# A two-layer mixer with 32 routed experts per layer: expert weights loaded by 512 rows instead of 256

## The chip, the core and the metric

The kernel runs on one core of one Trainium2 chip, in float32. Five engines work side by side: TensorE (PE, with its weight loads PEld), VectorE (DVE), ScalarE (ACT), GpSimd (POOL) and SyncE (SP), which here issues nearly all transfers from device memory into the on-chip buffers. Sixteen DMA engines carry the transfers out. The metric is device microseconds (us) of one execution. Before the change it is 1542.18 us, the median of three runs (1540.11 to 1542.83).

## What is computed

Two layers are run over 256 tokens `x` and 256 context tokens `ctx` of width 1024. Each layer has a mixer (layer 0 a gated recurrence beside a spatial gating unit, layer 1 an attention with compressed keys) and then a mixture of 32 experts with two experts per token. Layer 0's experts see all 512 tokens, layer 1's only the 256 of `x`. The change is in the experts:

```python
def expert_block(args):                       # of hier_moe
    xb, e = args
    g, u = jnp.split(xb @ w_gu[e], 2, axis=-1)
    return (jax.nn.silu(g) * u) @ w_dn[e]
# w_gu: (2, 32, 1024, 1024), w_dn: (2, 32, 512, 1024), both float32
```

One expert has 4 MB of gate and up weights and 2 MB of down weights, so a layer has 192 MB, and both layers 384 MB of the 495 MB that the kernel moves.

## The kernel before

`body` runs `even_layer`, `moe` for layer 0, `odd_layer`, and `moe` for layer 1. In `moe` each expert has room for 64 token rows (`CAP`); what does not fit is left to `overflow`, which runs only if a count read from the data is positive.

**Steps.** `step(p)` (L1118) handles experts 2p and 2p+1; there are 16 steps a layer. It does `gate_up` for the first expert (L908: eight slices of the 1024 inputs, the stationary operand a slice of the gathered tokens `xT`, the moving one a weight row for each partition, 512 columns into each half of a PSUM bank), then for the second, then either `gather` (L871, which collects the tokens of the next four experts by a matmul with one-hot rows) or `combine` (L1039, which adds the finished outputs of four experts to the tokens), then `turned` (transposes the hidden rows), and `down` (L1019). PE's order is the order of the code (`manual_schedule`); for the other engines a planner chooses the order from a simulated run, SP's transfers included.

**Loads.** A load (`load_to`, L833) is 1 MB: 256 rows of one expert, two neighbouring rows on each partition, so 8 KB in one piece on each of 128 partitions. Twelve loads make a step: four and four of gate and up, two and two of down. Load number i goes into a slot of the pool `turn[i % len(turn)]` (L825 to L830). The pools are `wpb` and `wpa` (two 1 MB slots each, which the mixers use too), `wxa` (five slots in layer 0, eight in layer 1, L710 and L1433), `wxb` (four), and in layer 1 one slot `xcp`, in which `ctx` lay: 13 slots in layer 0, 17 in layer 1. A slot can be loaded again when the last matmul that reads it has ended. In layer 0 the list is turned so that load 191 ends it, and load 0 lies in `wpa`.

**Channels.** Row f of the down weights belongs to hidden channel f. With two neighbouring rows on a partition, `gate_up` puts channels 0 to 255 into one half of its PSUM bank and 256 to 511 into the other (`"p (a c n) -> p c a n"`, L914), each as one run of columns, and `turned` takes every second column (`h[par][:, j:256:2]`, L935).

**The test in the middle.** After step 11 of layer 0 and step 5 of layer 1 (`MID`), the kernel tests whether `overflow` must run:

```python
i = len(loads)
while turn[i % len(turn)] is not wpa:
    i += 1
load_to(i)
n = nc.values_load(nx[0:1, 0:1], min_val=0, max_val=15)
with tc.If(n > 0):
    overflow(n)
```

So loads are taken up to, and without, the first one that would go into `wpa`, since `overflow` uses `wpa` for its own weights. Later loads stand behind the test in the program, and a `wpa` slot is free for them only when PE is past it.

Of the kernel before, what the change touches and what calls it, by code (L numbers as in the profile page):

```python
# [16 lines left out]
D = 1024  # L17
# [8 lines left out]
def body(ctx, tc, I, out, dbg=None, stop=None):  # L26
# [305 lines left out]
    def even_layer(HL, main):  # L332
# [6 lines left out]
        with ExitStack() as st:  # L339
# [370 lines left out]
            wst, wxa = open_wxa(0, 5)  # L710
# [26 lines left out]
            ahead.append(load(W_out[:, 512:1024], wxa[-1]))  # L737
# [72 lines left out]
    def moe(R, wxa, nwb, out=None):  # L810
# [5 lines left out]
        with ExitStack() as st:  # L816
# [8 lines left out]
            n_load = 6 * NE  # L825
            if l == 0:
                turn = [wpb] * 2 + [wpa] * 2 + wxa + [wxb] * nwb
                turn = [turn[(i - n_load) % len(turn)] for i in range(len(turn))]
            else:
                turn = [wpb] * 2 + [wpa] * 2 + wxa + [xcp] + [wxb] * nwb  # L830
            loads = []

            def load_to(n):  # L833

                for i in range(len(loads), min(n, n_load)):
                    p, j = divmod(i, 12)
                    e, j, src = (2 * p + j // 4, j % 4, I["moe_w_gu"]) if j < 8 else (2 * p + (j - 8) // 2, j % 2, I["moe_w_dn"])
                    w = turn[i % len(turn)].tile([128, 2, D], F32, name="w")
                    if i >= n_load - 4:

                        c = (i - n_load + 4) // 2
                        v = w.rearrange("p k (h n) -> p (k h) n", h=2)
                        for e in range(2):
                            nc.sync.dma_start(v[:, 2 * e:2 * e + 2],
                                              src[l, NE - 2 + e, j * 256:(j + 1) * 256, c * 512:(c + 1) * 512]
                                              .rearrange("(p k) n -> p k n", p=128))
                        loads.append(v)
                        continue
                    nc.sync.dma_start(w, src[l, e, j * 256:(j + 1) * 256, :].rearrange("(p k) n -> p k n", p=128))
                    loads.append(w)  # L850
# [20 lines left out]
            def gather(P, xT, q0=0, q1=4):  # L871
# [36 lines left out]
            def gate_up(xT, base, wg):  # L908
# [34 lines left out]
            def gate_up_both(xT, wg):  # L943

                gus = [Q("gu") for _ in range(2)]
                for j in range(4):
                    w_ = wg(j)
                    for par in range(2):
                        for k in (2 * j, 2 * j + 1):
                            w = w_[:, k % 2, :].rearrange("p (a c n) -> p c a n", a=2, c=2)  # L950
# [12 lines left out]
            def finish(hT, w, PT, ws, fg, z):  # L963
# [6 lines left out]
                for c in range(2):  # L970
                    cs_ = slice(c * 512, (c + 1) * 512)
                    for k in range(4):
                        for par in range(2):
                            mm(py[c][64 * par:64 * par + 64, :], hT[par][:, k // 2, k % 2, :],  # L974
                               w[2 * c + k // 2][:, 2 * par + k % 2, :], start=k == 0, stop=k == 3)
# [27 lines left out]
            def settle(hT, w, PT, ws):  # L1003
# [3 lines left out]
                for c in range(2):  # L1007
                    for k in range(4):
                        for par in range(2):
                            mm(py[c][64 * par:64 * par + 64, :], hT[par][:, k // 2, k % 2, :],  # L1010
                               w[2 * c + k // 2][:, 2 * par + k % 2, :], start=k == 0, stop=k == 3)
# [7 lines left out]
            def down(hT, wd, ws, gated=False):  # L1019

                py = [Q("dn") for _ in range(2)]
                for j in range(2):
                    w_ = wd(j)
                    for k in (2 * j, 2 * j + 1):
                        for c in range(2):
                            for par in range(2):
                                mm(py[c][64 * par:64 * par + 64, :], hT[par][:, k // 2, k % 2, :],  # L1027
# [450 lines left out]
```

## Time and profile before

| | |
|---|---|
| median of three runs | 1542.18 us |
| the profiled execution | 1538.64 us, of which 1536.9 us from first to last instruction |
| busy: PE, PEld, DVE, ACT, POOL | 93%, 54%, 43%, 28%, 15% of the span |
| moved | 495.22 MB, mean 322 GB/s |
| layer 0's experts | about 402 to 890 us |
| layer 1's experts | about 1074 to the end |

A busy PE counts matmuls whose ends are modelled, and neighbouring matmuls overlap in the trace. The 1.7 us between the profiled execution's time and its span lie around the instructions.

### The profile page before, as it was taken

How to read it: one execution, taken by the hardware profiler on the slowest of the kernel's cores; microseconds unless marked ns; L12 is line 12 of the kernel's file. 1: busy time of each engine (PE TensorE's matmuls, PEld its weight loads, DVE VectorE, ACT ScalarE, POOL GpSimd, SP SyncE). 2: the span in 40 equal slices, each digit the busy share in tenths (PEclk: the TensorE clock that was granted, in tenths of full speed). 3: DMA queues.
4: the chain of work that ended last, by engine and by line, in shares of the span. 5: the costliest groups of instructions: out<-in, count | busy, mean ns of one | idle time of the engine just before them, and what ended most of it. 6: DMA issues, size and time to landing. Idle time of an engine off the chain costs nothing. (4 is left out here: it accounts for less than half of the span.)

```text
span 1536.9 us, 21613 instructions
## 1 busy us (share of the span) xinstructions
PE 1435.8 (93%) x8526; PEld 836.2 (54%) x8526; DVE 662.7 (43%) x1494; ACT 432.5 (28%) x984; POOL 224.9 (15%) x250
## 2 busy tenths in 40 slices
PE   6989999999799999999999988997999989999987
PEld 5767777868444554554535356886344434334443
DVE  4455546767424334244423455666232323222222
ACT  4433334543111111211112144453122212212212
POOL 2222222123002012022203221101010100010010
PEclk9999999999899999999999999998999999999999
DMA  9775344785899999999899853135999999999995
GB/s 354 230 248 162 114 144 159 289 298 202 352 406 420 419 421 419 419 420 420 362 417 381 334 226 104 53 99 204 404 420 420 420 419 421 420 421 420 420 420 207
DMA packets 126051, 495.22 MB, mean 322 GB/s; under 512 B 17739, under 2 KB 38636, under 8 KB 77816
## 3 DMA queue, kind: packets, MB, share of 16 engines
q1 hardware_dynamic: 119704, 487.33, 80.3%
q10 hardware_dynamic: 2192, 3.72, 0.7%
q0 software_dynamic: 4048, 2.73, 0.6%
q8 instruction: 70, 1.15, 0.3%
q14 instruction: 37, 0.30, 0.1%
HBM read 492.59 MB, written 1.13 MB: 321 GB/s over the span
## 5 line engine op out<-in xcount | busy, mean ns | idle before, releaser
L916 PE MATMUL gu<-w,xT 128*64 128x512 f32 x2048 | 456.6, 597 | 19.1 <-DMA w<-in_moe_w_gu_dram 13.2
L916 PEld LDWEIGHTS gu<-w,xT 128*64 128x64 f32 x2048 | 151.6, 138 | 313.5 <-issue 273.6
L1027 PE MATMUL dn<-w,hh 128*64 128x512 f32 x960 | 220.2, 606 | 0.0
L924 DVE COPY hh<-gu 128x256 f32<-128x256 f32 x64 | 27.2, 425 | 363.2 <-ACT junk L923 363.2
L1050 POOL TENSOR_TENSOR xx<-xx,z 128x512 f32<-128x512 f32 x56 | 72.8, 1323 | 754.8 <-DVE z L1049 754.8
L1027 PEld LDWEIGHTS dn<-w,hh 128*64 128x64 f32 x960 | 73.7, 139 | 125.1 <-issue 117.9
L923 ACT ACTIVATE junk<-gu 128x256 f32<-128x256 f32 x64 | 24.5, 384 | 397.4 <-PE gu L916 397.4
L120 PE MATMUL mm<-WH,hH 128*128 128x512 f32 x288 | 116.5, 407 | 0.7 <-ACT hH L115 0.7
L121 PE MATMUL mm<-WL,hH 128*128 128x512 f32 x288 | 115.0, 400 | 1.4 <-DVE WL L116 1.4
L122 PE MATMUL mm<-WH,hL 128*128 128x512 f32 x288 | 112.0, 398 | 0.0
L1017 DVE SCALAR_TENSOR_TENSOR y<-dn,ws,y 128x512 fp32r<-128x512 f32 x60 | 45.0, 751 | 145.9 <-ACT y L1016 143.8
L1046 PE MATMUL ad<-y,PT 128*128 128x512 f32 x368 | 95.1, 405 | 5.3 <-DVE z L1049 4.2
L1016 ACT ACTIVATE y<-dn,ws 128x512 fp32r<-128x512 f32 x60 | 41.2, 687 | 176.2 <-PE dn L1027 166.1
L1046 PEld LDWEIGHTS ad<-y,PT 128*128 128x128 f32 x368 | 66.1, 188 | 35.9 <-issue 13.0
L116 DVE TENSOR_TENSOR WL<-w,WH 128x512 fp32r<-128x512 f32 x76 | 56.6, 752 | 54.9 <-ACT WH L115 51.5
L115 ACT ACTIVATE WH<-w 128x512 fp32r<-128x512 f32 x80 | 48.4, 627 | 109.9 <-PE mm L122 86.6
L1049 DVE TENSOR_TENSOR z<-ad,gt 128x512 f32<-128x512 f32 x100 | 66.1, 683 | 14.3 <-PE ad L1046 9.1
L399 PE MATMUL ad<-w,cst 128*32 128x128 f32 x1536 | 60.6, 284 | 6.7 <-DMA w<-in_ada_w_dram 6.7
L120 PEld LDWEIGHTS mm<-WH,hH 128*128 128x128 f32 x288 | 54.8, 190 | 16.9 <-issue 4.0
L121 PEld LDWEIGHTS mm<-WL,hH 128*128 128x128 f32 x288 | 54.8, 190 | 13.0 <-DVE WL L116 1.5
L122 PEld LDWEIGHTS mm<-WH,hL 128*128 128x128 f32 x288 | 54.1, 189 | 12.9 <-issue 1.6
L414 POOL DMA_DIRECT2D mod<-ada_r x80 | 40.4, 512 | 140.1 <-ACT ada_r L412 126.0
(434 smaller groups left out, 1962.3 us busy)
## 6 DMA issues: line engine op xcount, KB each, us to landing
w<-in_moe_w_gu_dram SPq DMA_DIRECT2D x256, 1024.0 KB, 16.3
w<-in_moe_w_dn_dram SPq DMA_DIRECT2D x120, 1024.0 KB, 12.2
w<-in_ada_w_dram SPq DMA_DIRECT2D x48, 1024.0 KB, 7.4
w<-in_ev_w_in_dram SPq DMA_DIRECT2D x32, 256.0 KB, 4.3
w<-in_moe_w_dn_dram SPq DMA_DIRECT2D x16, 512.0 KB, 12.0
w<-in_ev_w_in_dram SPq DMA_DIRECT2D x6, 1024.0 KB, 5.0
w<-in_ev_w_out_dram SPq DMA_DIRECT2D x4, 1024.0 KB, 6.9
w<-in_od_w_out_dram SPq DMA_DIRECT2D x4, 1024.0 KB, 5.1
```

The costliest lines, as they stand in the source:

```text
L115: act(H, src, AF.Copy)
L116: (eng or V).tensor_tensor(L, src, H, op=OP.subtract)
L120: mm(out, lh, rh, start=start, stop=False, skip_group_check=True)
L121: mm(out, lh, rl, start=False, stop=False, skip_group_check=True)
L122: return mm(out, ll, rh, start=False, stop=stop, skip_group_check=True)
L399: mm(pa[32 * j:32 * j + 32, 0:128], cst[:, k, :], w[k // 4][:, k % 4, j * 128:(j + 1) * 128], start=k == 0, stop=cols is not None and k == ...
L916: mm(gu[64 * c:64 * c + 64, :], xT[:, k, base:base + CAP], w[:, c], start=k == 0, stop=k == KC - 1)
L1017: V.scalar_tensor_tensor(y[:, 1], py, ws, y[:, 0], op0=OP.mult, op1=OP.subtract)
L1027: mm(py[c][64 * par:64 * par + 64, :], hT[par][:, k // 2, k % 2, :], w_[par][:, k % 2, c * 512:(c + 1) * 512], start=k == 0, stop=k == 3)
L1046: mm(cb, PT[:, t, :], y[c][:, i % 2], start=i == 0, stop=i == 2 * len(pend) - 1)
L1049: V.tensor_tensor(z, cb, gate[t // 2][:, hs_], op=OP.mult)
L1050: (V if n % 4 == 3 else nc.gpsimd).tensor_tensor(xs[t][:, hs_], xs[t][:, hs_], z, op=OP.add)
```

## The change

A load becomes 2 MB: 512 rows of one expert, four neighbouring rows on each partition, 16 KB in one piece. A step has six loads instead of twelve, and each has a slot of 2 MB. `wxa` has two such slots in layer 0 and four in layer 1, `wxb` two in each, `xcp` is no longer used for weights, and the two 1 MB slots of `wpb` and of `wpa` stand for one slot each; a load into them is two transfers of 8 KB pieces. That makes six slots (12 MB) in layer 0 and eight (16 MB) in layer 1. The order of pools begins with `wpb`, then `wpa`. The last two loads of a layer are cut by columns as before (pieces of 2 KB). Down weights of four neighbouring rows ask for another grouping of channels: column 4n + 2c + j of gate or up goes to half c. So `gate_up`'s moving operand is read in pairs of columns, two taken and two left, and `gather` takes every fourth column of the tokens as stationary operand instead of every second. The numbers and shapes of the matmuls do not change, nor do `MID` and the loop around the test.

```diff
-            wst, wxa = open_wxa(0, 5)
+            wst, wxa = open_wxa(0, 2)
...
-            ahead.append(load(W_out[:, 512:1024], wxa[-1]))
+            w = wxa[-1].tile([128, 8, 512], F32, name="w")
+            for i in range(2):
+                nc.sync.dma_start(w[:, 4 * i:4 * i + 4], W_out[i * 512:(i + 1) * 512, 512:1024].rearrange("(k p) n -> p k n", p=128))
+            ahead.append([w[:, 0:4], w[:, 4:8]])
...
-            n_load = 6 * NE
+            n_load = 3 * NE
+            turn = [wpb, wpa] + wxa + [wxb] * nwb
             if l == 0:
-                turn = [wpb] * 2 + [wpa] * 2 + wxa + [wxb] * nwb
                 turn = [turn[(i - n_load) % len(turn)] for i in range(len(turn))]
-            else:
-                turn = [wpb] * 2 + [wpa] * 2 + wxa + [xcp] + [wxb] * nwb
...
-                    p, j = divmod(i, 12)
-                    e, j, src = (2 * p + j // 4, j % 4, I["moe_w_gu"]) if j < 8 else (2 * p + (j - 8) // 2, j % 2, I["moe_w_dn"])
-                    w = turn[i % len(turn)].tile([128, 2, D], F32, name="w")
...
-                    nc.sync.dma_start(w, src[l, e, j * 256:(j + 1) * 256, :].rearrange("(p k) n -> p k n", p=128))
-                    loads.append(w)
+                    p, j = divmod(i, 6)
+                    e, j, src = (2 * p + j // 2, j % 2, I["moe_w_gu"]) if j < 4 else (2 * p + j - 4, 0, I["moe_w_dn"])
+                    pool = turn[i % len(turn)]
+                    small, end = pool is wpa or pool is wpb, i >= n_load - 2
+                    if end:
+
+                        c = i - n_load + 2
+                        halves = [src[l, NE - 2 + e, :, c * 512:(c + 1) * 512].rearrange("(p k) n -> p k n", p=128) for e in range(2)]
+                    else:
+                        v = src[l, e, j * 512:(j + 1) * 512, :].rearrange("(p k) n -> p k n", p=128)
+                        halves = [v[:, 0:2], v[:, 2:4]]
+                    m, n_ = halves[0].shape[1], halves[0].shape[2]
+                    if small:
+                        ws = [pool.tile([128, m, n_], F32, name="w") for _ in range(2)]
+                    else:
+                        w = pool.tile([128, 2 * m, n_], F32, name="w")
+                        ws = [w[:, 0:m], w[:, m:2 * m]]
+                    if small or end:
+                        for w_, h_ in zip(ws, halves):
+                            nc.sync.dma_start(w_, h_)
+                    else:
+                        nc.sync.dma_start(w, v)
+                    loads.append([w_[:, k, :] for w_ in ws for k in range(m)])
...
-                            mm(px[:, j, :], hs[t][:, part, 256 * (k // 2) + k % 2:256 * (k // 2) + 256:2], P[:, t, :],
+                            mm(px[:, j, :], hs[t][:, part, 512 * (k // 4) + k % 4:512 * (k // 4) + 512:4], P[:, t, :],
...
+            def halves_of(w):
+
+                return w.rearrange("p (a n c j) -> p c a n j", a=2, c=2, j=2)
+
-                for j in range(4):
-                    w_ = wg(j)
-                    for k in (2 * j, 2 * j + 1):
-                        w = w_[:, k % 2, :].rearrange("p (a c n) -> p c a n", a=2, c=2)
-                        for c in range(2):
-                            mm(gu[64 * c:64 * c + 64, :], xT[:, k, base:base + CAP], w[:, c],
-                               start=k == 0, stop=k == KC - 1)
+                for k in range(KC):
+                    w = halves_of(wk(k))
+                    for c in range(2):
+                        mm(gu[64 * c:64 * c + 64, :], xT[:, k, base:base + CAP], w[:, c],
+                           start=k == 0, stop=k == KC - 1)
...
-            moe(R, wxa, 4)
+            moe(R, wxa, 2)
...
-    wst, wxa = open_wxa(1, 8)
+    wst, wxa = open_wxa(1, 4)
```

`down`, `settle`, `finish` and `overflow` take the same rows from the new loads, `step` calls `load_to(6 * p + 6)` and takes six loads, and the modulation `R.mod` of layer 1 is laid out by four neighbouring channels.

## Rows read from the trace of the kernel before

**Rows 1.** The page's first line.

```profile
span 1536.9 us, 21613 instructions
```

**Rows 2.** Stretches: length, busy time of each engine, granted clock, DMA share, GB/s.

```profile
489.06:518.64 29.58, 29.58 (x170) 15.48 (x168) 6.24 (x14) 6.25 (x15) 0.00 (x0) 1.00 1.01 419
1150.48:1176.04 25.56, 25.56 (x136) 11.42 (x134) 6.68 (x15) 6.91 (x17) 0.00 (x0) 1.00 1.01 421
1400.00:1460.00 60.00, 54.55 (x256) 26.59 (x253) 16.29 (x34) 11.84 (x28) 3.94 (x3) 1.00 1.01 421
```

**Rows 3.** PE in order of time, one step of layer 0: start, length, what.

```profile
458.78 13.90 PE L916 MATMUL gu<-w,xT 128*64 128x512 f32 x64
472.61 6.65 PE L1046 MATMUL ad<-y,PT 128*128 128x512 f32 x28
...
481.53 7.09 PE L1027 MATMUL dn<-w,hh 128*64 128x512 f32 x32
```

**Rows 4.** PE in order of time, layer 1: first step, and near the end.

```profile
1073.70 13.96 PE L916 MATMUL gu<-w,xT 128*64 128x512 f32 x64
...
1471.85 1.94 PE L916 MATMUL gu<-w,xT 128*64 128x512 f32 x8 [0.56 <-DMA w<-in_moe_w_gu_dram]
```

**Rows 5.** The chain that ended last, two of its pieces in layer 1: start, length, what.

```profile
1456.95 19.82 DMA w<-in_moe_w_gu_dram
...
1494.56 8.71 PE gu L916 x32
```

**Rows 6.** SP's transfers in order of time, layer 1: first one after the full slots.

```profile
1075.68 0.33 SPq L849 DMA_DIRECT2D w<-in_moe_w_gu_dram  x1
```

**Rows 7.** DMA totals from 15 to 35 and from 1300 to 1360 us; page's instruction queue.

```profile
DMA packets 3897, 7.71 MB, mean 386 GB/s; under 512 B 148, under 2 KB 151, under 8 KB 3894
DMA packets 3459, 25.20 MB, mean 420 GB/s; under 512 B 385, under 2 KB 385, under 8 KB 385
q8 instruction: 70, 1.15, 0.3%
```

**Rows 8.** Weight loads of PE by line: count, shortest/median/longest ns, first and last start.

```profile
L213 PEld LDWEIGHTS bt<-ident,xx x32: 185/193/253, 359.5 to 1057.1; 128*128 128x128 f32 x32
L881 PEld LDWEIGHTS ad<-P,hH x256: 193/194/332, 392.8 to 815.7; 128*128 128x128 f32 x128
```

**Rows 9.** SP's transfers into `w`, 723 to 766.9 us, by kind; then the next one.

```profile
L849 SPq DMA_DIRECT2D w<-in_moe_w_gu_dram x8: 328/328/383, 726.4 to 738.0; - x8
L849 SPq DMA_DIRECT2D w<-in_moe_w_dn_dram x5: 327/328/387, 722.9 to 755.5; - x5
766.95 0.33 SPq L849 DMA_DIRECT2D w<-in_moe_w_dn_dram  x1
```

**Rows 10.** The test's line by engine, then PE in time order after layer 0's test.

```profile
L1177 PEldq EVENT_SEMAPHORE  x2: 51/51/51, 766.9 to 1232.0; - x2
...
767.13 13.95 PE L916 MATMUL gu<-w,xT 128*64 128x512 f32 x64 [3.22 <-PEq L1177]
785.41 8.78 PE L1027 MATMUL dn<-w,hh 128*64 128x512 f32 x32
```

**Rows 11.** One lone 1 MB load at 1036 us: issue to landing.

```profile
DMA to landing us min/median/max: 4.8/4.8/4.8
```

**Rows 12.** The stretch of that `down`, columns as in the second group.

```profile
785.41:794.02 8.61, 8.61 (x33) 2.73 (x34) 0.69 (x1) 1.27 (x3) 0.00 (x0) 0.80 1.01 417
```

**Rows 13.** SP's first 17 loads of layer 1, by kind: first and last start.

```profile
L849 SPq DMA_DIRECT2D w<-in_moe_w_gu_dram x13: 327/341/703, 878.9 to 1055.2; - x13
L849 SPq DMA_DIRECT2D w<-in_moe_w_dn_dram x4: 328/448/493, 880.9 to 884.4; - x4
```

More of the change, by code (lines that the diff above doesn't have):

```diff
@@ L835, in load_to @@
                 for i in range(len(loads), min(n, n_load)):
-                    p, j = divmod(i, 12)
-                    e, j, src = (2 * p + j // 4, j % 4, I["moe_w_gu"]) if j < 8 else (2 * p + (j - 8) // 2, j % 2, I["moe_w_dn"])
-                    w = turn[i % len(turn)].tile([128, 2, D], F32, name="w")
[L839 to L848, printed above, removed]
@@ L974, in finish @@
                             mm(py[c][64 * par:64 * par + 64, :], hT[par][:, k // 2, k % 2, :],
-                               w[2 * c + k // 2][:, 2 * par + k % 2, :], start=k == 0, stop=k == 3)
+                               w[c][4 * par + k], start=k == 0, stop=k == 3)
                     y.append(mo.tile([128, 512], F32, name="z", bufs=4))
@@ L1010, in settle @@
                             mm(py[c][64 * par:64 * par + 64, :], hT[par][:, k // 2, k % 2, :],
-                               w[2 * c + k // 2][:, 2 * par + k % 2, :], start=k == 0, stop=k == 3)
+                               w[c][4 * par + k], start=k == 0, stop=k == 3)
                     weighted(y[c], py[c], ws)
@@ L1017, in weighted, with down @@
                 V.scalar_tensor_tensor(y[:, 1], py, ws, y[:, 0], op0=OP.mult, op1=OP.subtract)
-            def down(hT, wd, ws, gated=False):
+            def down(hT, wk, ws, gated=False):
                 py = [Q("dn") for _ in range(2)]
[L1022 to L1027, printed above, removed]
-                                   w_[par][:, k % 2, c * 512:(c + 1) * 512], start=k == 0, stop=k == 3)
+                for k in range(4):
+                    w_ = wk(k)
+                    for c in range(2):
+                        for par in range(2):
+                            mm(py[c][64 * par:64 * par + 64, :], hT[par][:, k // 2, k % 2, :],
+                               w_[par][:, c * 512:(c + 1) * 512], start=k == 0, stop=k == 3)
                 y = [mo.tile([128, 2, 512], F32R, name=f"y{c}", bufs=2) for c in range(2)]
@@ L1104, in overflow, with down_rows @@
                     hT = turned(h)
-                    y = down(hT, lambda j: [chunk(I["moe_w_dn"], j)] * 2, ws)
+                    wd = {}
+                    def down_rows(k):
+                        if k % 2 == 0:
+                            wd[0] = chunk(I["moe_w_dn"], k // 2)
+                        return [wd[0][:, k % 2, :]] * 2
+                    y = down(hT, down_rows, ws)
                     combine([(y, PT)])
@@ L1120, in step @@
                 nonlocal xT, P
-                load_to(12 * p + 12)
-                w = loads[12 * p:12 * p + 12]
+                load_to(6 * p + 6)
+                w = loads[6 * p:6 * p + 6]
                 odd = p % 2
@@ L1129, in step @@
                 end = p == last and out is not None
-                h = [gate_up(xT, b, lambda j: w[j])]
+                h = [gate_up(xT, b, lambda k: w[k // 4][k % 4])]
                 if end:
@@ L1136, in step @@
                     PT, ws = back(Pw)
-                h.append(gate_up(xT, b + CAP, lambda j: w[4 + j]))
+                h.append(gate_up(xT, b + CAP, lambda k: w[2 + k // 4][k % 4]))
                 n = 2 * NT
@@ L1148, in step @@
                 if end:
-                    finish(hT, w[8:], PT, ws, fg, z)
+                    finish(hT, w[4:], PT, ws, fg, z)
                     return
@@ L1158, in step @@
                     gated = p == last - 1 and out is not None
-                    pend.append((down(hT, lambda j: (w[8 + j], w[10 + j]), ws, gated), PT))
+                    pend.append((down(hT, lambda k: (w[4][k], w[5][k]), ws, gated), PT))
                 else:
-                    settle(hT, w[8:], PT, ws)
+                    settle(hT, w[4:], PT, ws)
             P = one_hots(0)
@@ L1436, in body @@
         R = odd_layer(HL, main)
-        moe(R, wxa, 4, out)
+        moe(R, wxa, 2, out)
     wst.close()
```

12 lines of the change are left out of this document (6 added, 6 removed).

## The prediction

> **What bounds the kernel now.** I read the stretches first, then PE's order of time, the chain that ended last, SP's transfers, and last PE's weight loads. The expert stages of the two layers have different limits. A step of layer 0 takes 29.58 us, PE is busy in all of it at full clock, and the transfers run at 419 GB/s [rows 2]. Its parts are two experts' gate and up in 13.90 us, the combine of 6.65 (or the gather) and the down of 7.09, with transposes between [rows 3]. A step moves 12 MB, 12.58 million bytes, which at 420 GB/s take 29.96 us. So PE sets layer 0, and the transfers are only just quick enough. In layer 1 there are half as many tokens, a step needs 25.56 us of PE [rows 2], and the transfers still need 29.96. It begins with 17 MB in its slots, uses these up, and late in the layer PE waits before each load: 1.94 us of matmuls, then 0.56 us for the next [rows 4], and the chain runs through transfers [rows 5]. So the transfers set layer 1 up to step 14; from 1494.56 us the chain is PE's again [rows 5]. The reader is to see that "DMA 1.01" stands in both layers and means a limit only in the second.
>
> **The change part by part.**
>
> *Layer 1.* All of it hangs on when the transfers run without a break and how fast. They do so from 1075.68 us [rows 6], when the first 1 MB slot is free, 1.98 us after PE began [rows 4]. Four terms:
> - Sixteen MB lie ready instead of 17, so one MB more is to be moved after the start: 12.58 million bytes per 12 MB at 420 GB/s is 2.5 us a MB, +2.5 us.
> - The first slot is free after 2 MB instead of 1. A MB of gate and up is 8 of the 64 matmuls of 13.90 us [rows 3], 1.74 us: +1.7.
> - Where PE waits for a load, it has 2 MB of work left when that has landed, not 1: +1.7, once, at the last wait before PE's own tail.
> - The packets. From 15 to 35 us nearly all are 2 KB and the queue is full: 386 GB/s over 16 engines is 24.1 GB/s each, 85 ns a packet. From 1300 to 1360 us they are 8 KB: 420 GB/s, 312 ns [rows 7]. Four small ones take 340 ns where one large takes 312, so 28/3 = 9.4 ns a packet are fixed. A packet of 16 KB would take 2 x 312 - 9.4 = 615 ns, 426 GB/s, 1.5% faster. Six of eight slots get such packets, and 160 MB remain after the start: 160 x 2.5 x 0.75 x 1.5% = -4.5 us, or 3.0 us for each per cent.
>
> The sum is +1.4 us. The packets are the unknown: no transfer of weights here has 16 KB packets. Their gain lies between none (they are cut, and layer 1 loses 5.9 us) and the whole fixed share, 9.4 of 312 ns or 3% (layer 1 gains 3.1 us); I take the straight line, since two sizes give it. On the bad side the only packets of 16 KB in the trace are the instruction queue's, 1.15 MB in 70, at 0.3% of 16 engines' span, 0.003 x 16 x 1536.9 / 70 = 1.05 us each [rows 1, 7], 1.7 times the straight line; these are single ones among other traffic, so I keep them for a rival only.
>
> *Layer 0, steps 0 to 11.* Twelve MB of slots are exactly one step. Counted from a step's start, the two down slots are freed at 0 (by the step before), the four others at 3.5, 7, 10.4 and 13.9 us, and a slot's 2 MB take 5 us. With the queue never empty the downs land at about 12, the next step's loads at 17, 22, 27 and 32; they are needed at 22 and at 29.6, 33, 36.5 and 40. That is 8 us of room, of which 29.96 - 29.58 = 0.4 us go in each step: 11 steps leave over 3 us. PE stays the bound: 0 us, and faster packets give nothing here.
>
> *Layer 0, the test after step 11.* This is the largest term. Loads are taken up to the first that would go into `wpa`. Before, step 12's eight gate and up loads and three of its four downs leave by 755.5 us, 11 MB; the next goes at 766.95 [rows 9], right after PE's mark past the test at 766.9 [rows 10]. After the change, load 72 goes into `wpb` and load 73 is `wpa`'s: 2 MB. The queue then runs dry some 20 us before PE is past the test, and 10 MB of step 12 are issued at 767. A lone 1 MB lands 4.8 us after its issue [rows 11], each further one 2.5 us later: the halves of load 73 at 771.8 and 774.3, then 779.3, 784.3, 789.3, and the second down at 794.3. PE starts at 767.1 and has used load 72 at 770.6. It waits for the two halves, 773.5 and 776.0 after their work, then 782.8 and 787.8. The transposes take 4.4 us (the gap from the gate-up's end, 781.0, to 785.41 [rows 10]), so PE is at 792.2, and waits for the down until 794.3 instead of 785.41: +8.9 us. The transfers are then late by their whole room, and 29.96 against 29.58 us costs some 0.4 us a step, and the lost room about 1 us in step 13: +2. A pause drops PE's clock: after the idle time in step 12 the down takes 8.78 us instead of 7.09, at a granted clock of 0.80 of 2.4 GHz [rows 3, 10, 12], so part of the step at 1.2 GHz; I add 1. Together +12 us. Nothing later takes it up: PE's order runs on from here into layer 1's mixer, and the transfers of layer 1 that set its end begin when PE does [rows 4, 6].
>
> *Layer 1, the test.* Five loads, 10 MB, precede it. The first load after the start lands at 1075.68 + 1.7 + 4.8 = 1082, so by 1232, when PE passes the test [rows 10], 16 MB and (1232 - 1082)/2.5 = 60 more have landed; load 40 ends at MB 82, so the queue has work for 15 us beyond the test: 0 us.
>
> *Operand patterns.* `gate_up`'s moving operand is now read in pairs. The trace shows no moving operand with gaps, so the cost lies between nothing and a doubling of 13.9 us a step. A stationary with gaps is shown: the transposes of L213 take every eighth element and load in 193 ns, `gather`'s every second in 194 [rows 8]. `gather` with every fourth lies between: 0. For the moving operand the same two rows are the nearest, and I take 0. The Trainium skill says in "SBUF — State Buffer", at the cachelines note under "Door 1: The DMA port swizzle", that a read needs at least two hits in each 16-byte line to keep full bandwidth. By that rule the pairs, two hits a line, cost nothing, and `gather`'s stationary, one hit a line, would be slower, where before it had two; row L213, with less than one hit a line, loads as fast as the others, and the measurement decides.
>
> *Small things.* SP issues about half as many transfers; it is not what anyone waits for. The second half of `W_out` lies in one 2 MB slot, and 2 MB instead of 3 of experts' weights go out early; by 402 us all slots can be full either way.
>
> The sum is 12 + 1.4 = +13.4 us. The profiled execution takes 1538.64 us, so 1552.0; it lies 3.5 below the median of 1542.18, which with the same sum gives 1555.6. I say 1555 us.
>
> **The rivals.**
> - *The planner sends the unhindered loads ahead.* It does not keep program order: of layer 1's first 17 loads the four downs leave by 884.4, the last gate and up at 1055.2 [rows 13]. If after the test loads 74 and 75 (`wxa`, slots free near 735 and 739) and 76, 77 (`wxb`, 755) stand before 73, SP, which has only load 72 to issue before the test, can issue them while PE works towards it. They land before 767, load 73 at 771.8 and 774.3, and PE waits 1.2 + 0.8 us only. Total 2 + 1.4 = +3.4 us, 1545.6. Against it: behind a test, the order may be made as if all engines came there together, and then program order holds. I cannot see which.
> - *Faster than before: the packets gain more than the line says.* The place is layer 1's transfer chain, at 3.0 us a per cent. With the rival above, 2 + 5.9 - 3.0 x is below -3.1 us from x = 3.7% on; at 4% the time is 1538. With program order it needs 7%. Against it: the fixed share is 3% in all.
> - *Packets of 16 KB are slower.* At 5% slower on three quarters, layer 1 loses 15 + 5.9, and in layer 0 a step's transfers take 31 us against PE's 29.6, so about 1.4 x 16 less the 8 us of room, 14: with the test's 12 about +47, 1589.
> - *The reads in pairs are slower.* Doubled, each step has 13.9 us more of PE: 222 in layer 0, and in layer 1 (25.6 + 13.9 - 30) x 16 = 152: 1920. By the skill's line rule `gather` alone would suffer: its 512 loads in layer 0 doubled by 194 ns add up to 99 us, about 1655. Against both: rows 8.
>
> **How the numbers follow.** The forecast has 0.52, the planner's order 0.24, faster packets 0.12, slower packets 0.06, slower reads 0.06 (0.02 of them the line rule). A measurement of this kernel tells about 0.2% (3 us) from no change. The planner's case lies around that bound, half of it the same. Faster 0.12, same 0.12, slower 0.52 + 0.12 + 0.12 = 0.76. The forecast's own range is 1549 to 1564: the test from 9 to 16 us, packets from no gain to 3%. With the planner's case it goes down to 1541, and for a mixture with somewhat slower packets up to 1569.
>
> **What the profile after would show.** Right: a gap in the transfers of some 20 us before PE passes the first test, several waits of PE for gate and up weights in step 12, the rest of layer 0 at 29.6 us a step, gate and up still 13.9, and in layer 1 about 426 GB/s with 16 KB packets. Wrong: step 12 without waits (the planner), layer 1's rate far from 426, or a gate and up of more than 14 us.

## The result, and the profile after the change

The changed kernel takes 1627.54 us (median of four runs, 1625.33 to 1631.84), the kernel before, timed beside it, 1541.22: a ratio of 1.0559 with an interval of 1.0540 to 1.0578, 86 us slower. The forecast was 1555 us with a range up to 1569. The direction is right, but most of the time was not in my sum.

The page's first line of the kernel after, which answers to [rows 1], and the first line of its section on the chain that ended last (share of the span by engine):

```profile
span 1625.3 us, 21336 instructions
...
PE 17%; DVE 1%; ACT 0%; issue 0%; ACTq 0%; DVEq 0%
```

The chain no longer has a transfer in it, where before it ran through them late in layer 1 [rows 5]. The stretches of four steps, columns as in [rows 2]: layer 0 with a combine, layer 0 with a gather, and the same two kinds in layer 1.

```profile
472.05:502.41 30.36, 30.13 (x139) 13.60 (x137) 16.60 (x24) 5.17 (x13) 8.17 (x6) 1.00 0.97 400
502.41:540.06 37.65, 37.65 (x170) 22.73 (x168) 6.24 (x13) 6.25 (x15) 0.00 (x0) 1.00 0.84 347
1204.61:1231.50 26.89, 26.33 (x120) 10.51 (x118) 9.70 (x19) 4.95 (x13) 3.94 (x3) 1.00 1.01 425
1231.50:1261.30 29.80, 29.80 (x136) 14.86 (x134) 6.78 (x15) 6.98 (x17) 0.00 (x0) 1.00 1.01 424
```

Both steps of [rows 2] have a gather. They took 29.58 and 25.56 us; now they take 37.65 and 29.80, with PE busy in all of it at full clock. In layer 0 the transfers have fallen to 347 GB/s: they wait for PE to free their slots. PE in order of time shows which of its work has grown (start, length, what; the same kinds of parts as in [rows 3]):

```profile
465.13 7.09 PE L1037 MATMUL dn<-w,hh 128*64 128x512 f32 x32
...
502.41 14.60 PE L927 MATMUL gu<-w,xT 128*64 128x512 f32 x64
516.94 0.74 PE L890 MATMUL ad<-P,hH 128*128 128x256 f32 x2
517.52 0.64 PE L890 MATMUL ad<-P,hL 128*128 128x256 f32 x2
517.99 0.63 PE L890 MATMUL ad<-P,hH 128*128 128x256 f32 x2
```

The down is what it was. Two gate_ups take 14.60 us instead of 13.90. The gather, now L890, sends two matmuls every 0.47 us. Before it sent two every 0.24, as these lines of the kernel before show:

```profile
502.87 0.40 PE L881 MATMUL ad<-P,hH 128*128 128x256 f32 x2
503.11 0.41 PE L881 MATMUL ad<-P,hL 128*128 128x256 f32 x2
```

Its weight loads (shortest, median, longest ns) answer to the second line of [rows 8], where the median was 194:

```profile
L890 PEld LDWEIGHTS ad<-P,hH x256: 307/332/337, 390.7 to 884.8; 128*128 128x128 f32 x128
```

**Where the 88.4 us between the two spans lie.** I compared the start of each step's first gate_up in the two traces.

| stretch | before | after | more |
|---|---|---|---|
| start to the first step of layer 0 (first gather) | 402.36 | 405.95 | 3.6 |
| layer 0's first step to layer 1's first step | 671.3 | 740.3 | 69.0 |
| layer 1's first step to the end | 463.2 | 479.1 | 15.9 |

Of the 69.0 us, seven steps with a gather account for 7 x 7.4 = 52 (a step grew by 8.07, 0.70 of it gate_up), sixteen steps' gate_ups for 16 x 0.70 = 11, and the test for 2.7; the other 3 us are small differences in two steps and the mixer. The first gather of layer 0 took 15.0 us instead of 9.4, but began 2 us earlier; the first of layer 1 took 7.7 instead of 6.1. Both ran below full clock in the kernel before (0.80 and 0.61 granted). In layer 1, PE's work grew by 16 x 0.68 + 7 x 3.6 = 36 us after the first gate_up. Only 16 of it show, because the transfers set that layer before. The waits of PE in layer 1 of the kernel before (us in all, times, longest) had this line, and the same view of the kernel after has no wait for a weight:

```profile
PE gu L916 <- DMA w<-in_moe_w_gu_dram: 13.2, 23, 2.0
```

### The profile page after: what moved, and what is told of

It reads as the page before. It is cut to its first block, busy times and chain, and to the rows that moved or that the text cites. A ratio compares the mean times of both kernels' runs of the same rounds, so it can differ in the third digit from the quotient of the medians.

```text
span 1625.3 us, 21336 instructions
## 1 busy us (share of the span) xinstructions
PE 1537.7 (95%) x8526; PEld 909.0 (56%) x8526; DVE 660.8 (41%) x1494; ACT 434.1 (27%) x984; POOL 224.6 (14%) x250
## 5 line engine op out<-in xcount | busy, mean ns | idle before, releaser
L927 PE MATMUL gu<-w,xT 128*64 128x512 f32 x2048 | 471.4, 617 | 8.6 <-PEq L1194 6.0
L927 PEld LDWEIGHTS gu<-w,xT 128*64 128x64 f32 x2048 | 145.4, 135 | 324.6 <-issue 317.0
L1037 PEld LDWEIGHTS dn<-w,hh 128*64 128x64 f32 x960 | 67.7, 140 | 130.0 <-issue 130.0
L890 PE MATMUL ad<-P,hH 128*128 128x256 f32 x256 | 82.7, 405 | 1.6 <-DVE P L865 1.6
L890 PE MATMUL ad<-P,hL 128*128 128x256 f32 x256 | 81.3, 400 | 0.0
L890 PEld LDWEIGHTS ad<-P,hH 128*128 128x128 f32 x256 | 72.2, 330 | 7.7 <-issue 7.7
L890 PEld LDWEIGHTS ad<-P,hL 128*128 128x128 f32 x256 | 72.5, 332 | 0.0
```

The source lines that it names most:

```text
L890: mm(px[:, j, :], hs[t][:, part, 512 * (k // 4) + k % 4:512 * (k // 4) + 512:4], P[:, t, :], start=i == 0, stop=i == 2 * NT - 1)
```

## The experiments

Two theories stood against each other after the result. "Pattern": PE pays for how its operands lie, whatever is transferred. "Traffic": the landing of 16 KB packets slows PE's reads. The loads' own part of my sum was open under either. The experiments are called m1 and e1 to e10, as the expectations call them.

### The price of a pattern by itself (m1)

The kernel before, with groups of 16 matmuls after step 3 of layer 0. Nobody reads their results. In the edit, s stands for 4, 1, 2, 3, 5, 6, 7, 8 (for 8 the columns begin at 0); groups in other number formats are left out of the cut.

```diff
+                for i in range(16):
+                    mm(pa[:, 0:256], hs[i % 2][:, i // 2 % 2, s - 1:s - 1 + 128 * s:s], P[:, 0, 0:256], start=True, stop=True)
...
+                for i in range(16):
+                    tp(pa[:, 0:128], hs[i % 2][:, i // 2 % 2, ...].bitcast(F32), ident)
...
+                for i in range(16):
+                    for c in range(2):
+                        mm(pa[64 * c:64 * c + 64, :], xT[:, i % 8, 0:64], w_[:, i % 2, 0:512], start=True, stop=True)
```

> The kernel before with extra matmuls after step 3 of layer 0, whose results nobody reads: groups of 16 with one operand pattern each, so that the distance from one matmul to the next prices the pattern by itself, under 8 KB packets. Theory 'pattern' (PE pays for how its operands lie): a stationary operand of every fourth column with 256 moving columns goes at about 0.233 us a matmul, as the gather of the changed kernel does, one of every second or of neighbouring columns at 0.12; moving pairs of columns cost about 0.008 us more a matmul than neighbouring ones. What the eighth column costs is open: by the transposes of rows 8 it is as quick as the second, by a rule of one hit in 16 bytes every stride from four on is slow. Theory 'traffic' (PE's reads are slowed by the landing of 16 KB packets): all patterns alike, 0.12 us. The extra work adds some 90 us to the time.

The one run took 1699.1 us; the extra work costs 157 us where I expected 90, which bears on neither theory. PE in order of time, the first matmul of a group. The distance to the next group's first, divided by 16, is the price of one matmul. L1169 is every fourth column, then neighbours, every second, third and fifth, and after two groups that are not shown every eighth (L1183). From L1185 they are transposes with neighbours, every second, fourth and eighth column.

```profile
514.72 0.51 PE L1169 MATMUL ad<-P,hH 128*128 128x256 f32 x1
518.58 0.28 PE L1171 MATMUL ad<-P,hH 128*128 128x256 f32 x1
520.41 0.28 PE L1173 MATMUL ad<-P,hH 128*128 128x256 f32 x1
522.34 0.33 PE L1175 MATMUL ad<-P,hH 128*128 128x256 f32 x1
525.17 0.39 PE L1177 MATMUL ad<-P,hH 128*128 128x256 f32 x1
...
536.23 0.40 PE L1183 MATMUL ad<-P,hH 128*128 128x256 f32 x1
540.12 0.27 PE L1185 MATMUL ad<-ident,hH 128*128 128x128 f32 x1
541.86 0.28 PE L1187 MATMUL ad<-ident,hH 128*128 128x128 f32 x1
543.78 0.29 PE L1189 MATMUL ad<-ident,hH 128*128 128x128 f32 x1
545.72 0.28 PE L1191 MATMUL ad<-ident,hH 128*128 128x128 f32 x1
```

Neighbours cost 1.83 / 16 = 0.114 us a matmul, every second column 0.121, every third 0.177, every fourth 0.241 (0.233 between most of them), the fifth to the eighth 0.226 to 0.243. For transposes nothing of the kind: 0.109, 0.120, 0.121, 0.112. The weight loads of the matmuls say the same (every fourth, neighbours, every second, third and eighth; then the transpose of every fourth, and a float32 matmul of every fourth):

```profile
L1169 PEld LDWEIGHTS ad<-P,hH x8: 308/330/332, 514.7 to 518.0; 128*128 128x128 f32 x8
...
L1171 PEld LDWEIGHTS ad<-P,hH x8: 187/188/208, 518.4 to 520.1; 128*128 128x128 f32 x8
...
L1173 PEld LDWEIGHTS ad<-P,hH x8: 193/194/199, 520.3 to 522.0; 128*128 128x128 f32 x8
...
L1175 PEld LDWEIGHTS ad<-P,hH x8: 250/263/264, 522.2 to 524.7; 128*128 128x128 f32 x8
...
L1183 PEld LDWEIGHTS ad<-P,hH x8: 336/340/345, 536.1 to 539.5; 128*128 128x128 f32 x8
...
L1189 PEld LDWEIGHTS ad<-ident,hH x8: 211/212/213, 543.7 to 545.4; 128*128 128x128 f32 x8
...
L1197 PEld LDWEIGHTS ad<-P,hH x16: 308/332/332, 561.1 to 567.9; 128*128 128x128 f32 x16
```

The last line excludes a rival. The gather's matmuls are in the code's format F32R and the transposes in float32, so the number format could have made the difference. But a float32 matmul's weight load of every fourth column takes 332 ns too, so it is the operation.

And the moving operand, 64 matmuls as in two gate_ups: neighbouring columns, every second, every fourth, two of every four, four of every eight.

```profile
589.48 13.95 PE L1210 MATMUL ad<-w,xT 128*64 128x512 f32 x64
...
603.27 14.57 PE L1213 MATMUL ad<-w,xT 128*64 128x512 f32 x64
...
617.67 28.97 PE L1216 MATMUL ad<-w,xT 128*64 128x512 f32 x64
...
646.45 14.62 PE L1219 MATMUL ad<-w,xT 128*64 128x512 f32 x64
...
660.88 13.91 PE L1222 MATMUL ad<-w,xT 128*64 128x512 f32 x64
```

Both numbers of the changed kernel are here, 0.233 us a gather matmul and 14.6 us for two gate_ups, without one weight packet of 16 KB. "Traffic" is not needed for them.

### gather on neighbouring columns, in the changed kernel (e1)

```diff
+    def by4(x, j):
+        return x[:, 512 * j:512 * j + 512].rearrange("p (n k) -> p k n", k=4)
+    def slots(x, j):
+        return x[:, 512 * j:512 * j + 512].rearrange("p (k n) -> p k n", k=4)
...
-            split(h2, hs[:, 0, :], hs[:, 1, :])
+            for j in range(2):
+                split(by4(h2, j), slots(hs[:, 0, :], j), slots(hs[:, 1, :], j))
...
-hs[t][:, part, 512 * (k // 4) + k % 4:512 * (k // 4) + 512:4]
+hs[t][:, part, 128 * k:128 * k + 128]
```

> The changed kernel, but the rows of tokens are written to their tiles in the order in which gather takes them, so that its stationary operand is 128 neighbouring columns; same values, same loads. Theory 'pattern': layer 0 loses 3.6 us before its first step and 7.4 in each of 7 steps with a gather (55 us); in layer 1 eight gathers get 3.55 us shorter, but then the transfers (12.58 million bytes a step at 427 GB/s, 29.5 us) are the limit again and give only part of it: about 1560 us (1553 to 1568). Theory 'traffic': no change from 1627.

Measured: 1563.74 us, 1.0145 of before (1.0121 to 1.0169). So undoing the gather's stationary operand alone takes away 64 of the 86 us, as theory "pattern" had it, and theory "traffic" falls: the 16 KB packets are still there.

### gate_up in runs, in the changed kernel (e2)

```diff
-w.rearrange("p (a n c j) -> p c a n j", a=2, c=2, j=2)
+w.rearrange("p (a c n) -> p c a n", a=2, c=2)
...
+                    elif p6 >= 4:
+                        halves = [src[l, e, i * 256:(i + 1) * 256, :].rearrange("(p k) n -> p k n", p=128) for i in range(2)]
```

> The changed kernel with gate_up's moving operand in runs of 256 columns instead of pairs; for that the down weights lie in two neighbouring rows on a partition (8 KB packets for a third of the loads). gather keeps every fourth column. Theory 'pattern': a step's two gate_ups take 13.9 us instead of 14.6; layer 0 loses 16 x 0.7 = 11 us, layer 1, where a pair of steps then has 55.3 us of PE against 58.9 us of transfers and 16 MB lie ready, between 0 and 10: 1606 to 1617 us. If the half microsecond a step came from the packets and not from the pairs: 1620 us or more.

Measured: 1605.31 us, 1.0411 (1.0384 to 1.0437), 22 us below the changed kernel and just under my range: 32 x 0.7 = 22, so here layer 1 gives back all of its part. PE was its limit in the changed kernel, not the transfers.

### Both undone (e3)

The two edits above together.

> The changed kernel with both operand patterns taken back: gather as in e1, and gate_up's moving operand in runs of 256 columns, for which the down weights lie in two neighbouring rows on a partition (packets of 8 KB for a third of the loads; the rest keep 16 KB, and slots, order and test stay those of the change). Theory 'pattern': what is left is the loads' part of the prediction with the planner's order, +3.4 us, plus 2.75 us at the test: 1545 to 1550 us. Theory 'traffic': 1600 us or more.

Measured: 1555.2 us, 1.0072 (1.0048 to 1.0096). "Traffic" falls again, but the loads alone cost 5 to 10 us more than I expected. It is the forecast's number, and not by the forecast's terms, as the last experiments show.

The parts do not add up: 64 us for the gather, 22 for gate_up and 13 for the loads are 99, not 86. From layer 1's first step to the end the changed kernel takes 479.1 us, and e1, e2 and e3 take 469.5, 469.5 and 470.5. Either edit alone gives these 10 us back; with both, the transfers set the layer and nothing more comes of the second.

### gather on every fourth column, in the kernel before (e4)

```diff
+    def pairs(x, i):
+        return x[:, 256 * i:256 * i + 256].rearrange("p (n s) -> p n s", s=2)
+    def fours(x, i):
+        return x[:, 512 * (i // 2):512 * (i // 2) + 512].rearrange("p (n a s) -> p n a s", a=2, s=2)[:, :, i % 2]
...
-            split(h2, hs[:, 0, :], hs[:, 1, :])
+            for i in range(4):
+                split(pairs(h2, i), fours(hs[:, 0, :], i), fours(hs[:, 1, :], i))
...
-hs[t][:, part, 256 * (k // 2) + k % 2:256 * (k // 2) + 256:2]
+hs[t][:, part, 512 * (k // 4) + k % 4:512 * (k // 4) + 512:4]
```

> The kernel before with its own loads; only gather reads every fourth column (the rows of tokens are written in the order that makes this right). Theory 'pattern': layer 0 gets 3.6 + 7 x 7.4 = 55 us longer; in layer 1 a pair of steps has 25.6 + 26.2 + 3.6 us of PE, still below the 59.9 us of its transfers, so only the first gather and little else shows: 1597 to 1608 us. Theory 'traffic': 1541.

Measured: 1609.9 us (1598.39 to 1611.61), 1.042 (1.0378 to 1.0461): 68 us from one index expression, with no load changed. It is more than I expected, because layer 1 grew too. Its trace has 471.7 us from layer 1's first step to the end, against 463.2. The transfers hide most of the longer gathers there (7 x 3.6 = 25 us), not nearly all: PE waits for no weight any more.

### What the rewriting of the rows costs (e5, e8)

e1, e3 and e4 write the rows of tokens in another order, and e3's first step began 6.3 us late. So the kernel before got the rewriting alone, with gather on neighbouring columns:

```diff
+            for j in range(4):
+                split(by2(h2, j), slots(hs[:, 0, :], j), slots(hs[:, 1, :], j))
...
-hs[t][:, part, 256 * (k // 2) + k % 2:256 * (k // 2) + 256:2]
+hs[t][:, part, 128 * k:128 * k + 128]
```

> The kernel before with its own loads; the rows of tokens are written in an order in which gather reads neighbouring columns (in four pieces a tile, as in e4). This prices the rewriting that e1, e3 and e4 also carry. By e3's trace its first step starts 6 us late; the gather, 114 instead of 121 ns a matmul, gives back 7 x 0.45 = 3 us in layer 0; the mixer of layer 1 ends some 2 us late: 1543 to 1550 us. If the rewriting costs nothing: 1538 to 1541.

Measured: 1539.08 us, 0.9978 (0.9957 to 0.9999): the rewriting costs nothing, against what I expected. It looked even faster than before, so it was measured again, with 13 runs against 17 of the kernel before:

> The kernel of e5 again, in more rounds: loads of the kernel before, rows of tokens written so that gather reads neighbouring columns. e5's trace has seven gather steps of layer 0 shorter by 0.36 us and a first step 1.2 us later, a gain of 1.3 us by these, while its median lay 2.7 to 4.5 below: 1537 to 1542 us, 0.996 to 1.000 of before.

Measured: 1541.07 us, 0.9999 (0.9985 to 1.0013). No difference. The two traces of this one kernel show how far single executions differ: the first step of layer 0 begins at 403.58 in one and at 408.60 in the other, and the step after the test takes 26.89 and 31.04 us. From layer 1's first step to the end they take 463.2 and 467.7 us. A few microseconds in these places of one trace prove nothing about an edit.

### Layer 1 alone (e6)

Layer 0 from the kernel before, layer 1 with loads and patterns of the change.

```diff
-    wst, wxa = open_wxa(1, 8)
+    wst, wxa = open_wxa(1, 4)
...
-        moe(R, wxa, 4, out)
+        moe1(R, wxa, 2, out)
```

> Layer 0 and its test as in the kernel before, layer 1 as in the changed kernel, both operand patterns included. Theory 'pattern': the first gather ends 3.6 us later and nothing is loaded while it runs, after that the transfers set the pace of layer 1 (a pair of steps has 56.6 us of PE against 58.9 at 427 GB/s) apart from the time in which the 16 MB that lie ready are used up; with the prediction's +1.4 for the loads 1544 to 1552 us. If layer 1 stays bound by PE as in the changed kernel, whose layer 1 took 15 us more than before: 1553 to 1560.

Measured: 1559.18 us, 1.0096 (1.0073 to 1.0119). The second reading held. A stretch late in its layer 1 has PE busy in 59.4 of 60 us, against 54.55 in the third line of [rows 2]:

```profile
1320.00:1380.00 60.00, 59.42 (x270) 26.38 (x268) 17.03 (x37) 12.31 (x29) 3.95 (x3) 1.00 1.01 427
```

In the same line the transfers run at 427 GB/s, where [rows 7] has 420. The faster packets are there, and nobody waits for them. (Over 337 us of the layer the mean is 424.)

### The loads alone (e7)

The loads of the change with the operand patterns of the kernel before: gate_up as in e2, gather on every second column, for which the rows are written in small pieces.

```diff
+            for i in range(4):
+                split(fours(h2, i), pairs(hs[:, 0, :], i), pairs(hs[:, 1, :], i))
...
-hs[t][:, part, 512 * (k // 4) + k % 4:512 * (k // 4) + 512:4]
+hs[t][:, part, 256 * (k // 2) + k % 2:256 * (k // 2) + 256:2]
```

> As e3, the loads of the change without its operand patterns, but gather reads every second column as in the kernel before, and the rows of tokens are written for it in pieces that keep pairs of neighbours together. In e3 the first step began 6.3 us late, in e5, with its smaller pieces, 1.2. If that start and a part of layer 1's mixer are the rewriting's, this run gives the loads' own price: e3's 13.4 us less 5, about 1550 us (1546 to 1552), and my sum with the planner's order, 1545.6 plus 2.75 at the test, is right to 2 us. If e3's 13.4 us are the loads' own: 1553 to 1557.

Measured: 1553.85 us, 1.0086 (1.0066 to 1.0107), 13 us over before. The second reading held, and the rewriting is not the cause. Its trace repeats the kernel before to 0.05 us up to step 11 of layer 0. The test's wait is 2.4 us longer, and layer 1 takes 469.0 us instead of 463.2. The step after the test (3.9 us more) and layer 1's mixer (3.0) add the rest in this one trace; the first of these two is a place where the kernel above differs from itself by as much. So of the 13 us only the test's 2.4 and layer 1's part are followed up here; the rest stays open.

Layer 1's part is a pause. These are the stretches from 20 to 30 us after the layer's first gate_up, of the kernel before:

```profile
1093.70:1103.70 10.00, 10.00 (x50) 3.30 (x46) 1.50 (x2) 1.37 (x2) 0.00 (x0) 1.00 1.01 415
```

and of the loads alone:

```profile
1103.10:1113.10 10.00, 10.00 (x42) 3.15 (x40) 1.50 (x2) 1.37 (x2) 0.00 (x0) 0.84 0.55 197
```

PE in order of time, the down in that stretch of the loads alone:

```profile
1101.62 9.40 PE L1052 MATMUL dn<-w,hh 128*64 128x512 f32 x32
```

The transfers move 197 instead of 415 GB/s. The four gate and up slots have been refilled by then, and the next two slots come free only when both downs are through; with 1 MB slots half of the down was enough. The down itself takes 9.40 us at a lower clock, where [rows 3] has 7.09, so two causes are mixed. The trace of e4 has 1 MB slots and a down that is as slow, 9.83 us. The same 10 us of its layer 1:

```profile
1156.53:1166.53 10.00, 10.00 (x40) 3.15 (x38) 1.50 (x2) 1.37 (x2) 0.00 (x0) 0.81 0.79 311
```

So the slow clock alone brings 415 down to 311 GB/s, and the coarser slots take it on to 197: about half each. All other traces have this down below full clock; the trace of the kernel before is the exception. The next experiment takes away the slots' half.

### The small slots under the first down (e9)

```diff
+            else:
+                turn = wxa + [wpb, wpa] + [wxb] * nwb
```

> The kernel of e7 with the order of pools in layer 1 turned by four places, so that the two down loads of the first step lie in the slots made of two 1 MB tiles; half of each is free when half of the down is done, about 4 us before its end. In e7 the transfers pause there: from 20 to 30 us after the layer's first gate_up they move 197 GB/s, in the kernel before 415. Theory 'coarse slots': the pause gets some 3 to 4 us shorter, over 280 GB/s in those 10 us, and the time falls from e7's 1553.9 to 1549 to 1552. Theory 'only the lower clock of that down': the pause and the time stay.

Measured: 1556.81 us, 1.0094 (1.0074 to 1.0115); the time did not fall. The pause did go, as "coarse slots" said: the same 10 us move 419 GB/s, although the clock of that stretch is again below full (0.90; with 1 MB slots, e8 moves 348 GB/s at 0.89). But a new wait comes at layer 1's test. The stretch of the old pause, and one after the test:

```profile
1102.17:1112.17 10.00, 10.00 (x44) 3.32 (x42) 1.50 (x2) 1.37 (x2) 0.00 (x0) 0.90 1.02 419
...
1282.00:1296.00 14.00, 13.25 (x52) 4.17 (x52) 1.93 (x3) 2.51 (x6) 0.00 (x0) 0.77 0.52 195
```

PE's wait between the two, and SP's transfers around the test, in order of time:

```profile
1265.69 2.83 PE L944 MATMUL gu<-w,xT 128*64 128x512 f32 x6 [15.91 <-DMA w<-in_moe_w_gu_dram]
...
1238.08 0.80 SPq L875 DMA_DIRECT2D w<-in_moe_w_gu_dram  x2
1253.57 16.18 SPq L873 DMA_DIRECT2D w<-in_moe_w_gu_dram  x5
```

SP's waits from 1236 to 1256 us (us in all, times, longest):

```profile
SPq L1215 <- SPq L1215: 14.3, 6, 3.7
```

PE is past the test at 1244.73, but SP is held there for 14.3 us and sends its next load at 1253.57. With the pools turned, that load is the second one of the step that PE has begun: it goes into `wpa`, and all loads into `wpa` stand behind the test. PE waits 15.91 us for it. Then PE is late, so slots come free late, and the transfers pause after all, 195 GB/s from 1282 to 1296 us. In the kernel before SP is held at this test for as long, 14.7 us, but PE needs none of the loads behind it so soon. What a slot order gains in one place it can lose where the queue is held. What the pause costs in time this run cannot show, since the new wait covers it.

### Traffic at the test (e10)

```diff
+            if l == 0:
+                for q in range(4):
+                    scr = dram.tile([128, 2, D], F32, name=f"scr{q}")
+                    nc.sync.dma_start(scr, loads[i - 4])
             n = nc.values_load(nx[0:1, 0:1], min_val=0, max_val=15)
```

> The kernel before with four idle copies of 1 MB of weights from the chip to device memory, issued after the loads that precede layer 0's test, so that transfers are in flight while PE reaches the test; nobody reads the copies. In the kernel before the queue is dry from 762 us and PE's wait at the test is 3.2 us; in the changed kernel loads are in flight and it is 6.0. Theory 'the branch waits for a transfer of its own that stands behind the others': 5 to 7 us here too, the time some 3 us longer. If the longer wait has another cause: 3.2 us.

The run gives no answer. The planner put the copies behind the test (776.74 us), and PE's wait stayed at 3.48 us. The 1555.48 us of the one run come from step 13, which waited behind the copies. What can be said is a comparison over all traces. PE's branch at layer 0's test takes 3.5 to 4.5 us in six kernels with the loads of before in layer 0, and 5.8 to 6.2 in the six with those of the change. Layer 1's takes 0.33 us in all twelve. m1, with the loads of before, has 3.4 us at layer 0's test and 6.0 at layer 1's, so a branch of 6 us needs no larger loads. The lines of the kernel before and of the kernel after (both layers' tests; the longest is layer 0's):

```profile
L1177 PEldq COMPARE_BRANCH  x2: 333/1915/3497, 763.3 to 1230.5; - x2
```

```profile
L1194 PEldq COMPARE_BRANCH  x2: 332/3285/6238, 820.5 to 1320.7; - x2
```

The stretches of three long branches, columns as in [rows 2]: the kernel before, the kernel after, and layer 1's test in m1. Then the instruction queue's line for the second of them (packets, MB, share of 16 engines):

```profile
763.30:766.80 3.50, 0.61 (x3) 0.17 (x1) 2.30 (x3) 0.00 (x0) 3.50 (x3) 1.00 0.12 47
...
820.50:826.74 6.24, 0.53 (x3) 0.09 (x1) 2.23 (x3) 0.00 (x0) 3.54 (x3) 0.64 0.59 251
...
1392.90:1398.90 6.00, 1.36 (x7) 0.78 (x5) 3.44 (x4) 0.00 (x0) 3.30 (x3) 1.00 1.00 414
...
q8 instruction: 1, 0.02, 1.0%
```

The traces fit the theory that the branch waits for a transfer of its own. Each of the fourteen long branches has one such 16 KB packet of the instruction queue in it, and the twelve short ones have none. The branch ends 1.4 to 1.5 us after its packet. What differs is how late the packet starts: 1.0 to 2.0 us after the branch where 7 to 193 GB/s move, 3.4 to 3.8 us where 251 to 414 move. In the changed kernel the two 2 MB loads that SP sends at 812.64, when step 11's down has freed their slots, are still landing. That the branch waits for this packet is read from the traces; no run changed it by itself.

## Why the prediction was wrong, point by point

**The step that failed: "`gather` with every fourth lies between: 0".** It was worth 7.4 us in each of seven gathers of layer 0 and 3.6 in each of seven in layer 1, less in the first of either layer; taken back alone (e1), it gives 64 us of the 86. I bounded a matmul's stationary operand by L213, every eighth column at 193 ns [rows 8]. L213 is a transpose. The first experiment shows that a transpose costs nearly the same at any distance of the columns (0.109 to 0.121 us), while a matmul's weight load goes from 188 to 194, 263 and 330 ns for neighbours, every second, third and fourth. The row was near in pattern and far in operation. Between two rows of different operations there is no "between".

The Trainium skill, in "SBUF — State Buffer", at the cachelines note under "Door 1: The DMA port swizzle", asks for two hits in each 16-byte line, and I called it contradicted. For the stationary operand it holds here: two hits a line 194 ns, one hit 330. For the moving operand it doesn't say enough: two hits a line cost 14.6 us instead of 13.95, whether as pairs or as every second column, and one hit 28.97.

**"For the moving operand ... I take 0".** It was 0.70 us a step, 22 us in all by e2. My bounds, nothing and a doubling, did hold it. My sign of being wrong, a gate and up of more than 14 us, came.

**"PE stays the bound" in layer 0, steps 0 to 11.** Right for the loads. With the old patterns the changed loads give the same steps to 0.05 us.

**"The transfers set layer 1".** Right for the loads, wrong for the changed kernel: PE's added 36 us used up the room, and e6 has PE busy throughout. I never asked how much PE time layer 1 could take before it changes hands.

**The test in layer 0, +12 us.** Wrong in mechanism. It was the rival that the planner sends the unhindered loads ahead. SP's transfers at the test of the kernel after (loads 72, 74 with 75, 76 with 77, then 73):

```profile
776.80 2.13 SPq L856 DMA_DIRECT2D w<-in_moe_w_gu_dram  x2
785.84 3.93 SPq L858 DMA_DIRECT2D w<-in_moe_w_gu_dram  x2
812.64 0.81 SPq L858 DMA_DIRECT2D w<-in_moe_w_dn_dram  x2
826.83 0.83 SPq L856 DMA_DIRECT2D w<-in_moe_w_gu_dram  x2
```

PE waits for no load in step 12. What the test does cost is 2.7 us of PE's branch, which neither case had; by the traces an instruction packet starts late behind the loads in flight (e10):

```profile
827.00 3.68 PE L927 MATMUL gu<-w,xT 128*64 128x512 f32 x8 [5.97 <-PEq L1194]
```

**Layer 1's loads, +1.4 us.** With the loads alone it is +5.8 in the trace. That is rough: four traces in which the changed loads set the layer take 469.0 to 470.5 us from its first step to the end, four with the loads of before 463.2 to 467.7. Term by term: "The first slot is free after 2 MB" failed, since `wpb` is two tiles of 1 MB; the first refill leaves 1.98 us after PE's start, as before [rows 4, 6], so 0 instead of 1.7. The pause under the first down is the term that I had not looked for: 10 us at 197 instead of 415 GB/s are (415 - 197) x 10 / 420 = 5.2 us, and by e4 some 2.7 of them are the slots' and 2.5 the clock's. One MB more is 2.5, which no run shows by itself. "Where PE waits for a load, it has 2 MB of work left" held in kind: PE goes on in groups of 16 matmuls instead of 8,

```profile
1482.08 3.65 PE L942 MATMUL gu<-w,xT 128*64 128x512 f32 x16 [1.34 <-DMA w<-in_moe_w_gu_dram]
```

but the +1.7 is not shown: from the last landing of weights to the end it is 19.9 us instead of 18.3, and with the loads of before it is 17.4 in e5 and 20.0 in e8. The packets held. With a half of the loads at 16 KB the transfers run at 423 GB/s against 420 over the next 166 us of both traces, 0.7%, which is 160 x 2.5 x 0.7% = 2.8 us; my line from two packet sizes gives 423. In the changed kernel, with three quarters, they run at 425 over 337 us, where the line gives 425. (The 160 MB are low: 192 less the 16 that lie ready are 176, which changes the packets' term by 0.5 us.) With 2.5 + 5.2 + 1.7 - 2.8 = 6.6 the terms are near the 5.8, but single traces cannot tell more.

**The test in layer 1, 0 us.** Right for the changed kernel, whose transfers run at 418 GB/s or more there. e9 shows that it is not free: there SP, held for 14.3 us, sent the one load that PE needed next too late.

**The chances.** Slower had 0.76 and came true, but luckily: by a case that held little of it. The case that came true, slower reads, had 0.06, and the line rule in it 0.02, with 99 us for layer 0's gathers (measured: 55). I let one row outweigh a rule that spoke against the change. The forecast's 13.4 us and the 13 us of the loads alone agree by accident: 12 of the 13.4 lay at a test that took 3.

No run here beats the kernel before. The gain of the 16 KB packets is real but small, and it lies in a layer where the coarser slots cost more.

## What to carry to other kernels

Price a new access pattern by a row of the same operation, operand and number format. If there is none, keep the far bound in the range with a chance that counts, above all where an edit of one index touches hundreds of matmuls. Before calling a layer bound by transfers, add up how much more PE time it can take. When slots get coarser, follow the queue through the first steps slot by slot: the cost is where several slots come free at once.

## What the runs showed of the hardware

- A matmul's stationary operand of 128 columns loads in 188 ns from neighbouring columns, 194 from every second, 263 from every third, 330 from every fourth and 340 from every eighth. With 256 moving columns the matmul goes from 0.114 to 0.24 us. Transposes of the same tile stay between 0.109 and 0.121 us whatever the distance.
- A moving float32 operand read in runs of four columns costs nothing (13.91 us against 13.95), in pairs 5% (14.62), every fourth column twice the time (28.97). In the format F32R with 256 columns, pairs and every second column already cost nearly twice: 0.23 us a matmul instead of 0.13 (groups L1201 to L1207 of m1).
- Weights with three quarters in packets of 16 KB and the rest in 8 KB land at 424 to 425 GB/s over 337 us where 8 KB alone give 420.
- A test on a loaded value holds SP's queue: 14.3 us in e9, 8.8 of them after PE had gone on, and 14.7 in the kernel before.
- PE's branch at such a test took 0.33 us with no packet of the instruction queue in it, and 3.4 to 6.2 us with one. That packet started 1.0 to 2.0 us after the branch where up to 193 GB/s were moving, and 3.4 to 3.8 us after it where 251 or more were.
